# A gated layer's input projection, from plain products to a 2x2 block scheme with seven products

## The chip, the cores and the metric

The kernel runs on one core of a Trainium2 chip. The metric is the device time of one execution, in microseconds; the median of three runs is given. The trace is that of one execution taken by the hardware profiler. Of the core's engines, TensorE (PE) multiplies matrices into PSUM, VectorE (DVE), ScalarE (ACT) and GpSimd (POOL) work on elements, and SyncE (SP) issues the DMA transfers.

## The reference

Two batches, 512 "prompt" and 1024 "sample" tokens of 1024 features, go through two layers and a final norm. The first layer is multi-head latent attention. The second, which the change touches, is a chunked gMLP:

```python
def gmlp_layer(x, g, w_in, ln_g, ln_b, w_s, b_s, w_out):
    h = rmsnorm(x, g)
    u, v, gate = jnp.split(h @ w_in, 3, axis=-1)        # w_in: 1024 x 6144
    u = jax.nn.gelu(u, approximate=False)
    v = layernorm(jax.nn.gelu(v, approximate=False), ln_g, ln_b)
    vc = v.reshape(bsz, nc, 128, 8, 256)
    sv = jnp.einsum('gpq,bnqgd->bnpgd', w_s, vc) + jnp.transpose(b_s)[:, :, None]
    s = u * sv.reshape(bsz, seq, 2048)
    return x + (s * jax.nn.silu(gate)) @ w_out          # w_out: 2048 x 1024
```

All data is float32. Each large product is made of three: an operand is split into a rounded part (fp32r, "hi") and the remainder ("lo"), and hi*hi, hi*lo and lo*hi are summed in PSUM.

## The kernel before

Activations lie with features on the 128 partitions and tokens along the free axis. The 1536 tokens of the second layer ("layer B") are worked in three groups of 512: groups 0 and 1 are the sample batch, group 2 the prompt. The output projection of the attention layer (`AOut`, L719) writes its result to DRAM tiles `x1d`, one [128, 512] tile for each group and each of the eight feature tiles, and sums squares for the norm. `out_s` does groups 0 and 1, `out_p` (eight weight units of 24 products) group 2.

For each group, layer B then runs these stages:

- `b_prep` (L776): 1/rms of each token is spread over the partitions by small products (`start0`, `start`); `one(k)`, eight of them, loads a feature tile of `x1d` into a temporary (five buffers, tag `tmp`), scales it (L791) and splits it into `h2h` and `h2l`. Group 0's preparation is placed between the units of `out_p`, that of a later group between those of the output projection before it.
- `b_v` (L800): the 2048 features of v, with tokens on the partitions: the split activations are the stationary operand, weights of 512 columns the moving one; four column blocks x four units x four token tiles x two feature tiles x three products. Gelu, layer-norm statistics and the normalised v (`v2`) stay in SBUF.
- `b_ug` (L847): the 16 feature tiles of u and the 16 of the gate, in pairs: 24 products of 512 columns each (`mm3`, L132 to L134), then Gelu or Silu (L862). After each pair, `sp` (L866) mixes v over positions by small float32 products (L870), multiplies by u and gate and splits the result (`sf`).
- `b_out` (L887): output projection, 8 feature tiles x 48 products (L939 to L941), residual, squares; its final norm (`fin0` to `fin2`) is placed between steps of the next group's `b_v`.

Weights come as units of 512 KB (128 x 1024 float32) through the class `Weights` (L29): the DMA into `w_raw` (L43), rounded part by ACT (L50), remainder by DVE (L51), three buffers each. Units are split two ahead of use and loaded up to two ahead of that. Every DMA is issued on SP's queue.

The code is a list of steps (`step`, L113) that gives each instruction a priority; a planner then sets the order on each engine's queue, by what it expects to be ready, and each queue runs in that order, with a waiting instruction holding what stands behind it. Tiles share a fixed number of buffers by tag, and a new tile waits for a buffer of its tag. A pool that is opened after another is closed may lie on its addresses; its tiles then wait for those they overlap.

Of the kernel before, what the change touches and what calls it, by code (L numbers as in the profile page):

```python
# [22 lines left out]
C = 512  # L23
# [4 lines left out]

class Weights:  # L29
    """Stream of weight units: DRAM -> SBUF -> rounded part and remainder."""  # L30
# [8 lines left out]
    def _load(self, i):  # L39
        src = self.srcs[self.order[i]]  # L40
        n = src.shape[-1]
        t = self.pool.tile([128, 1024], F32, tag="w_raw", bufs=3, name="w_raw")
        self.nc.sync.dma_start(out=t[:, :n], in_=src)  # L43
        self.raw[i] = t, n
# [31 lines left out]
def trunk_kernel(tc, A):  # L76
# [24 lines left out]
    for d in range(16):  # L101
        srcs["wbu", d] = A["wbu"][d]
        srcs["wbg", d] = A["wbg"][d]
    for c in range(4):
        for u in range(4):
            srcs["wbv", c, u] = A["wbv"][c, u]
# [4 lines left out]
    prog = []          # (weight keys, function)  # L111
# [4 lines left out]
    st = {}            # state shared between steps  # L116

# [1 line left out]
    def mm_tile(name="mm"):  # L119
        return st["ps"].tile([128, C], F32, tag="mm", bufs=4, name=name)  # L120
# [7 lines left out]
    def mm3(out, terms):  # L128
        """sum of lhsT.T @ rhs over terms of (lhs hi, lhs lo, rhs hi, rhs lo)."""
# [54 lines left out]
    # the same in fewer dependent steps  # L184
# [36 lines left out]
    def setup():  # L221
        st["W"] = Weights(nc, open_pool("w", side="right"), srcs, order, 1, 3)
        st["ps"] = open_pool("psum", space=bass.MemoryType.PSUM)
# [11 lines left out]
        st["mhalf"] = const.tile([128, 4], F32, name="mhalf")  # L235
        dve.memset(st["mhalf"], -0.5)
        st["vec"] = const.tile([128, N_VEC], F32, name="vec")
# [16 lines left out]
    class AIn:  # L254
        """Input projection: latents (normalised, split), rotary key, gates."""
# [190 lines left out]
    def a_in_p(first):  # L446
        """-> (preparation steps, projection steps)"""
# [726 lines left out]
```

## Time and profile before

| | us |
|---|---|
| median of 3 runs | 2018.3 (2017.72 to 2018.39) |
| span of the profiled execution | 2016.2 |
| what lies around the span, taken from the two above | 2.1 |
| PE busy, share of the span | 1994.0, 99% |
| DVE busy | 1086.4, 54% |
| ACT busy | 813.4, 40% |
| DMA: bytes moved | 181.21 MB, mean 90 GB/s |

The profiled execution's own time is its span, 2016.2 us, and what lies around it, some 2.1 us. A busy PE is counted from the start of a product to its modelled end; products overlap, so the cost of one in a stream is the distance from start to start, and that is read from the order in time, not from the mean duration.

### The profile page before, as it was taken

Reading aid. Unit: us, or ns where it says so; the run is one execution under the profiler, and the core shown is the slowest. Engines: PE = TensorE matmul, PEld = TensorE weight load, DVE = VectorE, ACT = ScalarE, POOL = GpSimd, SP = SyncE. Lnnn points to the kernel's source line nnn. Section 1 sums busy time; section 2 is a strip of 40 time slices with the busy share of each in tenths; the row PEclk is TensorE's granted clock in tenths of the full one; section 3 lists DMA queues with packets and bytes.
Section 4 is the critical chain, followed back from the end, with each engine's and each line's share of the span. In section 5 each row is a group of like instructions: output and inputs, shape, how many; then the busy total and the mean of one; then the engine's idle time right before and its main releaser. Section 6 shows DMA issues by size and latency. Waiting matters only on the chain.

```text
span 2016.2 us, 24819 instructions
## 1 busy us (share of the span) xinstructions
PE 1994.0 (99%) x9984; PEld 1684.2 (84%) x9984; DVE 1086.4 (54%) x1580; ACT 813.4 (40%) x1207; POOL 134.4 (7%) x100
## 2 busy tenths in 40 slices
PE   8999999999999999999999999999999999999998
PEld 6888888888888888888888888888888888888887
DVE  7533777777856886255443445434444553434333
ACT  5323544545644654233244433323443332344421
POOL 4100000000110000220000001000000110000011
PEclk9999999999999999999999999999999999999999
DMA  4211000001113112463222234422223443222232
GB/s 157 84 44 55 22 18 16 22 21 38 48 53 107 53 61 86 143 216 121 94 94 94 87 107 157 141 95 94 93 84 105 146 142 109 94 94 84 94 120 100
DMA packets 65635, 181.21 MB, mean 90 GB/s; under 512 B 8048, under 2 KB 11632, under 8 KB 65520
## 3 DMA queue, kind: packets, MB, share of 16 engines
q1 hardware_dynamic: 65520, 179.63, 26.7%
q8 instruction: 78, 1.28, 0.3%
q14 instruction: 37, 0.30, 0.0%
HBM read 163.08 MB, written 12.58 MB: 87 GB/s over the span
## 4 chain that ended last, share of the span: by engine, by line
PE 95%; DVE 3%; issue 1%; ACT 1%; DMA 0%; POOL 0%; SPq 0%; POOLq 0%; DVEq 0%; ACTq 0%
PE mm L132 16%; PE mm L134 16%; PE mm L133 16%; PE s L581 9%; PE mm L941 4%; PE mm L940 4%; PE mm L939 4%; PE pst L613 3%; PE mm L828 2%; PE mm L826 2%; PE mm L827 2%; PE sv L870 2%; PE big L828 2%; PE big L826 2%; PE big L827 2%; PE o L133 2%
## 5 line engine op out<-in xcount | busy, mean ns | idle before, releaser
L51 DVE TENSOR_TENSOR w_lo<-w_raw,w_hi 128x1024 fp32r<-128x1024 f32 (+2 forms) x259 | 311.6, 1203 | 514.8 <-ACT w_hi L50 414.3
L50 ACT CAST w_hi<-w_raw 128x1024 fp32r<-128x1024 f32 (+2 forms) x259 | 266.4, 1029 | 643.2 <-PE mm L133 221.7
L132 PE MATMUL mm<-h2h,w_hi 128*128 128x512 f32 x768 | 300.9, 392 | 0.0
L134 PE MATMUL mm<-h2h,w_lo 128*128 128x512 f32 x768 | 298.9, 389 | 0.0
L133 PE MATMUL mm<-h2l,w_hi 128*128 128x512 f32 x768 | 298.8, 389 | 0.0
L212 POOL TENSOR_TENSOR acc<-acc,sq 128x512 f32<-128x512 f32 x70 | 107.9, 1542 | 1509.8 <-ACT sq L210 918.5
L134 PEld LDWEIGHTS mm<-h2h,w_lo 128*128 128x128 f32 x768 | 144.1, 188 | 30.4
L133 PEld LDWEIGHTS mm<-h2l,w_hi 128*128 128x128 f32 x768 | 144.2, 188 | 29.3
L132 PEld LDWEIGHTS mm<-h2h,w_hi 128*128 128x128 f32 x768 | 144.2, 188 | 29.2
L939 PE MATMUL mm<-sh,w_hi 128*128 128x512 f32 (+1 forms) x416 | 155.5, 374 | 0.0
L941 PE MATMUL mm<-sh,w_lo 128*128 128x512 f32 (+1 forms) x416 | 155.1, 373 | 0.0
L940 PE MATMUL mm<-sl,w_hi 128*128 128x512 f32 (+1 forms) x416 | 155.1, 373 | 0.0
L596 ACT ACTIVATE p<-s,sm 128x1024 f32<-128x1024 f32 (+1 forms) x96 | 93.2, 973 | 103.7 <-DVE sm L592 103.6
L132 PE MATMUL mm<-h_hi,w_hi 128*128 128x512 f32 x288 | 113.7, 395 | 1.1 <-ACT rbc L296 0.9
L137 ACT CAST pth<-pst 128x512 fp32r<-128x512 f32 x160 | 86.4, 590 | 67.2 <-PE pst L613 65.2
L134 PE MATMUL mm<-h_hi,w_lo 128*128 128x512 f32 x288 | 112.3, 390 | 0.0
L133 PE MATMUL mm<-h_lo,w_hi 128*128 128x512 f32 x288 | 112.1, 389 | 0.0
L138 DVE TENSOR_TENSOR ptl<-pst,pth 128x512 fp32r<-128x512 f32 x160 | 104.7, 682 | 8.4 <-ACT pth L137 8.3
L590 DVE TENSOR_REDUCE sm<-s 128x1 f32<-128x1024 f32 (+1 forms) x80 | 97.5, 1219 | 19.5 <-PE s L581 19.4
L133 PE MATMUL o<-ptl,vh 128*128 128x256 f32 x320 | 91.1, 285 | 0.0
L134 PE MATMUL o<-pth,vl 128*128 128x256 f32 x320 | 91.0, 284 | 0.0
L132 PE MATMUL o<-pth,vh 128*128 128x256 f32 x320 | 90.2, 282 | 0.0
(220 smaller groups left out, 3901.6 us busy)
## 6 DMA issues: line engine op xcount, KB each, us to landing
w_raw<-wbo SPq DMA_DIRECT2D x50, 512.0 KB, 3.6
w_raw<-wbv SPq DMA_DIRECT2D x48, 512.0 KB, 3.7
w_raw<-wbu SPq DMA_DIRECT2D x48, 512.0 KB, 3.6
w_raw<-wbg SPq DMA_DIRECT2D x48, 512.0 KB, 3.6
w_raw<-wa SPq DMA_DIRECT2D x25, 512.0 KB, 3.5
x<-x SPq DMA_DIRECT2D x48, 256.0 KB, 2.9
x<-xs SPq DMA_DIRECT2D x32, 256.0 KB, 3.1
w_raw<-wao SPq DMA_DIRECT2D x16, 512.0 KB, 3.8
```

The lines of the kernel that those rows point to most:

```text
L50: self.nc.scalar.copy(hi[:, :n], raw[:, :n])
L51: self.nc.vector.tensor_tensor(out=lo[:, :n], in0=raw[:, :n], in1=hi[:, :n].bitcast(F32), op=ALU.subtract)
L132: pe.matmul(out, lh, rh, start=(i == 0), stop=False)
L133: pe.matmul(out, lh, rl, start=False, stop=False)
L134: pe.matmul(out, ll, rh, start=False, stop=(i == n - 1))
L138: dve.tensor_tensor(out=lo, in0=src, in1=hi.bitcast(F32), op=ALU.subtract)
L212: pool_e.tensor_tensor(out=acc, in0=acc, in1=s, op=ALU.add)
L581: pe.matmul(s[:, j2 * C:(j2 + 1) * C], l[:, o], r[:, cc], start=(j == 0), stop=(j == 4))
L590: dve.tensor_reduce(out=sm[:, 0, :], in_=s.rearrange("p (a b) -> p a b", a=ns), axis=AX.X, op=ALU.max)
L939: pe.matmul(ps, wh[:, ksl(kk)], sh, start=(k == 0), stop=False)
L940: pe.matmul(ps, wh[:, ksl(kk)], sl, start=False, stop=False)
L941: pe.matmul(ps, wl[:, ksl(kk)], sh, start=False, stop=(k == 15))
```

## The change

The input projection of layer B is made of 2x2 blocks: the contracted features are halved (512 and 512), the output features are halved, and the tokens are halved. The four output blocks then come from seven block products of sums and differences of blocks, not from eight plain ones. The tokens are worked in two groups of 768 (so that half a group, `H`, is 384).

- The seven left factors are A11, A12, A22 of the weights and four sums S1 to S4. The sums don't depend on tokens; `w_sums(u)` makes them on the chip, 24 times: it loads 1 MB of weights into one tile, makes four [128, 512] results on DVE and stores 1 MB to DRAM. Four of these stand between the units of `out_p`, 14 in the first group's v stage, 6 in its u and gate stage.
- The seven right factors are made by `b_prep`, now four steps `one(k)` for each group: two loads of 768 tokens, one after the other through one buffer (`hx`), two scalings into `hQ` (one buffer), four subtractions of 384 columns, a store of three factors to DRAM (`gbd`), a split of the other four (1536 columns). `b_prep2` reloads and splits the three during v.
- `b_v`: for each group two halves of features, seven products, four feature tiles, three token tiles, three matmuls: 504 of 512 columns. `b_ug`: 16 units x 7 x 4 x 3 = 1344 of 384 columns.
- `gather` puts the products together: three of the seven are copied by ACT out of PSUM while the bank goes on being summed into (`held`), three results are the sum of a bank and such a copy (DVE).
- v goes to DRAM and comes back normalised for each pair of feature tiles (`load_v`); s goes to DRAM (`sd`) and is loaded and split in groups of 512 tokens for the output projection (`s_load`), whose first two feature tiles are interleaved by halves.
- PSUM has two tags of four banks in layer B.
- A weight unit is now two pieces of [128, 512]; 84 units for each group (168 in all, where there were 144), some loaded by two DMAs.

Of the diff, the new parts that carry work (`...` marks what is left out):

```diff
+    def w_sums(u):
+        def fn():
+            raw = st["ws"].tile([128, 4, C], F32, tag="ws_raw", bufs=1, name="ws_raw")
+            sm = st["ws"].tile([128, 4, C], F32, tag="ws_sum", bufs=1, name="ws_sum")
...
+            nc.sync.dma_start(out=raw, in_=src)
+            for o, a, b, op in ((sm[:, 1], raw[:, 2], raw[:, 3], ALU.add),
+                                (sm[:, 0], sm[:, 1], raw[:, 0], ALU.subtract),
+                                (sm[:, 2], raw[:, 0], raw[:, 2], ALU.subtract),
+                                (sm[:, 3], raw[:, 1], sm[:, 0], ALU.subtract)):
+                dve.tensor_tensor(out=o, in0=a, in1=b, op=op)
+            nc.sync.dma_start(out=dst, in_=sm)
+    def b_prep(G):
...
+        def one(k):
+            def fn():
+                Q = st["hq"].tile([128, 7, H], F32, tag="hQ", bufs=1, name="hQ")
+                for j in range(2):
+                    x = st["hq"].tile([128, 2 * H], F32, tag="hx", bufs=1, name="hx")
...
+                        nc.sync.dma_start(out=x[:, t0 - 2 * H * G:t0 - 2 * H * G + n],
+                                          in_=st["x1d", g, k + 4 * j][:, o:o + n])
...
+                    dve.scalar_tensor_tensor(
+                        out=Q[:, j:j + 5:4, :], in0=x.rearrange("p (a b) -> p a b", a=2),
...
+                for o, a, b in ((3, 4, 0), (2, 5, 3), (4, 5, 4), (6, 1, 2)):
+                    dve.tensor_tensor(out=Q[:, o, :], in0=Q[:, a, :], in1=Q[:, b, :], op=ALU.subtract)
+                nc.sync.dma_start(out=st["gbd", G, k], in_=Q[:, 4:7, :].rearrange("p a b -> p (a b)"))
...
+                split(hl[0], hl[1], Q[:, 0:4, :].rearrange("p a b -> p (a b)"))
...
+    def gather(i, ps, keep, new, n, sink):
+        X, Y, Z = (ps.get(r) for r in "XYZ")
+        def held(src):
+            t = new("t")[:, :n]
+            act.copy(t, src[:, :n])
+            return t
+        if i == 0:
+            keep["t1"] = held(X)
+        elif i == 1:
+            sink(0, 0, keep.pop("t1"), Y[:, :n])
+        elif i == 2:
+            keep["t2"] = held(X)
+        elif i == 3:
+            keep["t5"] = held(Z)
+        elif i == 4:
+            sink(1, 1, keep.pop("t5"), X[:, :n])
+        elif i == 5:
+            sink(0, 1, keep.pop("t2"), Z[:, :n])
+        else:
+            sink(1, 0, None, X[:, :n])
...
+        def unit(n, func, outs):
...
+                    for k in range(4):
+                        chain3(banks[BANK[i]][:, :H], (wh[:, ksl(k)], wl[:, ksl(k)]), right(i, k),
+                               k == 0 and i in (0, 1, 3), k == 3)
+                    gather(i, banks, keep, new, H, sink)
...
-    prep = [b_setup] + b_prep(0) + [b_bias(0), b_bias(1)]
+    prep = [b_setup] + b_prep(0) + [w_sums(i) for i in range(4)] + [b_bias(0), b_bias(1)]
...
-        for _ in range(2 if f else 0):
+        for _ in range(3 if f else 0):
             if prep:
                 step(prep.pop(0))
...
+    todo_w = list(range(4, 24))
+    for G in range(2):
+        step(open_in)
+        v, prep2 = b_v(G), b_prep2(G)
+        for i, s in enumerate(v):
+            step(*s)
+            if i % 4 == 3 and prep2:
+                step(prep2.pop(0))
+            if G == 0 and i % 4 == 1 and todo_w:
+                step(w_sums(todo_w.pop(0)))
+        step(open_ug)
...
+        for g in ((0,), (1, 2))[G]:
+            for d in range(16):
+                step(s_load(g, d))
+            fin = b_out(g, b_prep(1) if g == 0 else (list(fin) if g == 2 else []), g == 2)
```

The banks of the seven products are `BANK = "XYXZXZX"`: X is summed into by products 0, 2, 4 and 6, with a copy (0, 2) or an addition (4) that reads it in between.

## Rows read from the trace of the kernel before

**Rows 1.** Page, parts 1 and 4: span; shares of the chain that ended last.
```profile
span 2016.2 us, 24819 instructions
...
PE 95%; DVE 3%; issue 1%; ACT 1%; DMA 0%; POOL 0%; SPq 0%; POOLq 0%; DVEq 0%; ACTq 0%
```

**Rows 2.** Stages by windows: length, busy us (instructions) by engine, PE clock, DMA share, GB/s.
```profile
862.00:907.00 45.00, 45.00 (x198) 36.83 (x197) 28.34 (x38) 17.03 (x24) 12.48 (x10) 1.00 0.64 220
911.00:998.00 87.00, 87.00 (x386) 71.98 (x385) 38.29 (x57) 27.21 (x35) 2.94 (x4) 1.00 0.34 112
998.00:1186.60 188.60, 188.60 (x898) 158.44 (x897) 81.64 (x97) 80.27 (x95) 1.88 (x1) 1.00 0.27 90
1186.60:1273.60 87.00, 87.00 (x385) 72.02 (x384) 44.03 (x49) 26.80 (x34) 10.00 (x6) 1.00 0.43 145
2001.40:2016.20 14.80, 6.04 (x49) 5.68 (x47) 5.86 (x16) 0.42 (x1) 0.71 (x1) 0.78 0.41 142
```

**Rows 3.** Groups by shape: line, engine, tiles, count, busy us, mean ns, idle before.
```profile
L132 PE MATMUL mm<-h2h,w_hi 128*128 128x512 f32 x768 | 300.9, 392 | 0.0
L133 PEld LDWEIGHTS mm<-h2l,w_hi 128*128 128x128 f32 x768 | 144.2, 188 | 29.3
L870 PE MATMUL sv<-wsT,v 128*128 128x128 f32 x384 | 46.7, 275 | 0.0
```

**Rows 4.** Chain in order of time (start, us, what): two mixes, one pair apart, group 0.
```profile
1019.66 1.78 PE sv L870 x16
...
1043.24 1.78 PE sv L870 x16
```

**Rows 5.** PE in order of time: first and last of 21 products of 256 columns.
```profile
299.93 0.28 PE L132 MATMUL mm<-w_hi,lat4h 128*128 128x256 f32 x1
...
302.33 0.28 PE L134 MATMUL mm<-w_hi,lat4l 128*128 128x256 f32 x1
```

**Rows 6.** Groups by shape, DVE and ACT: what the new element work resembles.
```profile
L51 DVE TENSOR_TENSOR w_lo<-w_raw,w_hi 128x1024 fp32r<-128x1024 f32 x235 | 289.8, 1233 | 513.5 <-ACT w_hi L50 413.2 <-PE sv L870 99.8
L50 ACT CAST w_hi<-w_raw 128x1024 fp32r<-128x1024 f32 x235 | 247.1, 1052 | 620.4 <-PE mm L133 200.8 <-issue 188.5 <-PE mm L940 100.8
L137 ACT CAST pth<-pst 128x512 fp32r<-128x512 f32 x160 | 86.4, 590 | 67.2 <-PE pst L613 65.2 <-DVE qr L547 1.8
L879 DVE TENSOR_TENSOR sv<-sv,ug 128x512 f32<-128x512 f32 x48 | 30.9, 685 | 0.0
```

**Rows 7.** POOL, SP and DVE in order of time: norm factor, a load of `one(k)`, its scaling.
```profile
880.76 0.19 POOL L750 COPY r<-rstd 128x4 f32<-128x4 f32 x1
...
882.08 0.37 SPq L790 DMA_DIRECT2D x<-x  x1
...
885.20 0.75 DVE L791 SCALAR_TENSOR_TENSOR x<-x,vec,rbc 128x512 f32<-128x512 f32 x1 [2.19 <-DMA x<-x]
```

**Rows 8.** PE in order of time: where `out_p` ends and v begins.
```profile
909.09 0.39 PE L134 MATMUL mm<-goh,w_lo 128*128 128x512 f32 x1
...
909.77 0.80 PE L826 MATMUL big<-w_hi,h2h 128*128 128x512 f32 x1
```

**Rows 9.** DMA issues (count, KB each, median us to landing) and the densest window.
```profile
w_raw<-wbv SPq DMA_DIRECT2D x48, 512.0 KB, 3.7
x<-x SPq DMA_DIRECT2D x48, 256.0 KB, 2.9
...
890.00:900.00 10.00, 10.00 (x45) 8.27 (x45) 8.52 (x10) 4.82 (x7) 1.91 (x2) 1.00 0.80 269
```

**Rows 10.** DVE in order of time at the end of group 0's `b_ug`.
```profile
1189.28 1.29 DVE L880 TENSOR_TENSOR sv<-sv,ug 128x512 f32<-128x512 f32 x2
1190.48 0.69 DVE L180 TENSOR_TENSOR dg<-ident,r 128x512 f32<-128x512 f32 x1
1191.08 1.29 DVE L138 TENSOR_TENSOR sl<-sv,sh 128x512 fp32r<-128x512 f32 x2
```

**Rows 11.** Waits of SP's queue: the longest in total (us, times, longest).
```profile
SPq L43 <- DVE w_lo L51: 1409.2, 244, 38.1
```

More of the change, by code (lines that the diff above doesn't have):

```diff
@@ L40, in _load @@
         src = self.srcs[self.order[i]]
-        n = src.shape[-1]
+        parts = src() if callable(src) else [src]
         t = self.pool.tile([128, 1024], F32, tag="w_raw", bufs=3, name="w_raw")
-        self.nc.sync.dma_start(out=t[:, :n], in_=src)
+        n = 0
+        for a in parts:
+            self.nc.sync.dma_start(out=t[:, n:n + a.shape[-1]], in_=a)
+            n += a.shape[-1]
         self.raw[i] = t, n
@@ L794, in fn, with b_prep2 @@
+                st["ga", k] = hl
+            return fn
+        return [rb0(0), rb0(1), rb1(0), rb1(1)] + [one(k) for k in range(4)]
+    def b_prep2(G):
+        def one(k):
+            def fn():
+                x = st["h2b"].tile([128, 3 * H], F32, tag="gbx", bufs=1, name="gbx")
+                nc.sync.dma_start(out=x, in_=st["gbd", G, k])
+                hl = [st["h2b"].tile([128, 3 * H], F32R, tag=f"gb{e}{k}", bufs=1, name="gb" + e)
                       for e in "hl"]
                 split(hl[0], hl[1], x)
-                st["h2", k] = hl
+                st["gb", k] = hl
@@ new lines, in b_prep2, with right, bank, chain3 @@
+        return [one(k) for k in range(4)]
+    def right(i, k, o=slice(0, H)):
+        t, j = (st["ga", k], i) if i < 4 else (st["gb", k], i - 4)
+        return [a[:, j * H + o.start:j * H + o.stop] for a in t]
+    def bank(role):
+        return st["ps"].tile([128, C], F32, tag="x" if role == "X" else "y", bufs=4, name=role)
+    def chain3(ps, lhs, rhs, first, last):
+        (lh, ll), (rh, rl) = lhs, rhs
+        pe.matmul(ps, lh, rh, start=first, stop=False, skip_group_check=True)
+        pe.matmul(ps, lh, rl, start=False, stop=False, skip_group_check=True)
+        pe.matmul(ps, ll, rh, start=False, stop=last, skip_group_check=True)
@@ new lines, in mix, with end, fn @@
+            return fn
+        def end(p, u, g):
+            def fn():
+                for e in range(2):
+                    dve.tensor_tensor(out=u[e], in0=u[e], in1=g[e], op=ALU.mult)
+                    nc.sync.dma_start(out=st["sd", G, 2 * p + e], in_=u[e])
+            return fn
+        step(load_v(0))
+        for p in range(8):
+            u, g = [], []
+            unit(2 * p, AF.Gelu, u)
+            if p < 7:
+                step(load_v(p + 1))
+            for e in range(2):
+                step(mix(p, u, e))
+            unit(2 * p + 1, AF.Silu, g)
+            step(end(p, u, g))
@@ new lines, in s_load, with fn @@
+    def s_load(g, d):
+        def fn():
+            x = tmp("s")
+            t0 = g * C
+            while t0 < (g + 1) * C:
+                G, o = divmod(t0, 2 * H)
+                n = min(2 * H - o, (g + 1) * C - t0)
+                nc.sync.dma_start(out=x[:, t0 - g * C:t0 - g * C + n], in_=st["sd", G, d][:, o:o + n])
+                t0 += n
+            hl = [st["po"].tile([128, C], F32R, tag=f"s{e}{d}", bufs=1, name="s" + e) for e in "hl"]
+            split(hl[0], hl[1], x)
+            st["sf", d] = hl
+        return fn
@@ L970, in b_out @@
                     step((lambda: half_norm(0, st["hsq"])) if u == 0 else lambda: half_scale(0))
-            for e in extra[:1 if i < 2 else 2]:
-                step(e)
-            extra = extra[1 if i < 2 else 2:]
+                for e in extra[:1]:
+                    step(e)
+                extra = extra[1:]
         if last:
@@ L1055, in open_b3 @@
         close_pool("outp")
         close_pool("gatep")
-        st["b3"] = st["ap"] = open_pool("b3")
-        st["acc_n"] = 2
-    step(open_b3)
-    for g in range(3):
-        if g:
-            v = b_v(g)
-            for i in range(3):
-                steps(v[i:i + 1])
-                step(fin[i])
-            steps(v[3:])
-        b_ug(g)
-        fin = b_out(g, b_prep(g + 1) if g < 2 else [], g == 2)
+        close_pool("psum")
+        st["ps"], st["mm"] = open_pool("psumb", space=bass.MemoryType.PSUM), "y"
```

354 lines of the change are left out of this document (226 added, 128 removed).

## The prediction, as put on record before the changed kernel ran

> **What bounds the kernel now.** First the page: the span, and the chain that ended last, of which PE holds 95% [rows 1]; DVE has 3%, DMA none. Then the windows by stage [rows 2]: in v (911 to 998), u and gate (998 to 1186.6) and output (1186.6 to 1273.6) PE is busy for the whole stretch at the full granted clock, DVE for 43 to 51% of it, and the DMA engines for 27 to 43%. So in layer B a product less is its time less, as long as nothing else becomes late. The exception to keep in mind is the stretch just before v, 862 to 907: DVE is busy for 28.3 of 45 us and the DMA share is 0.64 [rows 2]. That is the place with the least cover, and the change puts work there.
>
> **What a product costs.** The order in time gives it. Two mixes stand one pair apart, at 1019.66 and 1043.24, and the mix takes 1.78 [rows 4]; the 96 products of 512 columns between them take 21.80 us, 0.2271 each. Products of 256 columns start 2.40 us apart over 20 steps, 0.1200 each [rows 5]. The 384 columns of the new u and gate products are not in the trace; midway between the two it is 0.1736, and I take that, since both neighbours lie on the same slope (0.42 ns a column and 13 ns fixed).
>
> **What the products give.** u and gate: 3 x 768 = 2304 of 512 columns before [rows 3], 523.2 us; after, 2 x 1344 = 2688 of 384, 466.6 us; 56.6 less. v: 1152 of 512 columns before, 1008 after, 144 x 0.2271 = 32.7 less. The mixes stay 384 instructions, and the output projection stays. Together **89.3 us**, all of it on the path. The rest of the sum is how much of that is lost to stalls of PE.
>
> **The new preparation, ahead of v.** `one(k)` now forms a chain, since its load and its result have one buffer each. The factor for group 1 is ready at 880.95, and spread over partitions some 3.5 us later [rows 7]: start 884.5. Per k, by the nearest rows: the scaling of 768 columns 1.1 (0.75 for 512), the second load 3.5 (3.1 from issue to scaling for 256 KB), a second scaling 1.1 [rows 7], four subtractions of 384 columns 4 x 0.55 (0.685 for 512 and 1.233 for 1024 give 1.07 ns a column) [rows 6], the store of 576 KB 3.8 [rows 9], beside which the split runs (ACT 1.5 and DVE 1.8 by [rows 6]), and 0.4 between engines: 12.1 us until the next k may write. The last k's split parts are there at 884.5 + 3 x 12.1 + 11.4 = 932. PE has finished `out_p` and begins v at 910 [rows 8]; its first product needs k = 0 to 3 in turn, and the fourth is due 27 products later, at 916. That is a stall of 16 us, and the lower end. The DMA engines make it longer: in its densest window the trace has 269 GB/s at a share of 0.80 [rows 9], 336 GB/s if all are busy. The stretch 862 to 907 moved 220 x 45 us = 9.9 MB [rows 2]; the change adds four weight sums at 2.1 MB, 2.4 MB of stores and 1 MB of loads, 21.7 MB or 65 us in a stretch of 48. With loads of 7 and stores of 8 us behind that queue a k takes 19.8 and the stall is 44. I take 4.5 and 5.5 (the queue is not full all the time): 14.8 for each k, ready at 941, a stall of **25 us** (16 to 44). PE waits in pieces there. The one idle end of the trace shows what the clock then does: a mean of 0.78 in 2001 to 2016, with PE busy for 6 of 14.8 us [rows 2], so partly at the lower level, 1.2 GHz. If the 27 products between the waits run at half speed that is 6 us; I take **3** (0 to 6).
>
> **The weight sums under v and u.** 24 sums, each a load of 1 MB (2.0 us fixed from a 512 KB load's 3.7 [rows 9], and 3.1 of moving: 5.1), 4 x 0.685 on DVE, and a store. From `out_p` to the end of the first group's u and gate stage PE has about 46 + 114 + 255 = 415 us of work (8 x 24 products and small ones; 504; 1344 and half the mixes). DVE has there: `out_p` and preparation 48; v 28 x 1.23 of weight remainders, 42 x 0.69 of additions and statistics, 5 of reloads: 69; u and gate 56 x 1.23, 48 x 0.55, 32 x 0.56 and 32 x 0.96 of mixing, 14 of normalising: 158; the sums 66. That is 341 of 415, with 74 idle. If the sums are ready when DVE comes to them, nothing is lost; if each holds DVE's queue for its load, 24 x 5.1 = 122, less the 74 idle, 48 are lost. Weights need not starve: their loads mostly wait for a free buffer now, 1409 us in all [rows 11], so they come early and have a reserve. In v the DMA engines would be asked for 14.7 MB of weights, 6.3 of v, 2.4 of factors and, if as fast as written, 29 of sums, 157 us at 336 GB/s against 114 of PE; but sums for u are not due until u, and may lag by 100 us. I take **10 us** (0 to 48), nearest to the present rows, where the planner's order leaves DVE little waiting for DMA.
>
> **Hand-overs in PSUM.** X is summed into again one product after it was read, so ACT's copy (or DVE's addition) has 12 x 0.1736 = 2.08 us. The copy of 384 columns takes about 0.48 (0.590 for 512), and one cast of a weight unit ahead of it 1.05 [rows 6]: 1.5 with 0.3 of hand-over is 1.8. It fits, with no more than one such piece ahead; in v the window is 8.2. Small losses are within the next item.
>
> **The changes of stage.** At each end of u and gate, s goes through DRAM: a store, a load and a split, 8 us for the last tiles, which are due only 2 x 24 products = 10.9 us into the output stage thanks to the interleaved halves; the early tiles lie on buffers in use to the end, 3 to 4 us. From v to u about 1, twice; the final norm of group 0 has no step of v written between its parts (0 to 5, since the planner may start v's products meanwhile); four buffers for six held copies in v, about 1 us four times. Sum **10 us** (3 to 25).
>
> **The sum.** The profiled execution: 2016.2 - 89.3 + 25 + 3 + 10 + 10 = 1974.9, and the 2.1 us by which the median stands above this span: **1977 us**. Its own range is 1950 to 2013: the low end has the 16 and the 3 and little else, the high end two of the upper bounds at once.
>
> **Rivals.**
> *The queues hold what waits at their heads; slower.* If the order on DVE and SP is close to the order of the code, each `one(k)` (12.4 with its loads behind a waiting store) and each of the first four sums (5.1 + 2.75 + half a store, 11) runs one after the other, and the weight remainders of `out_p`'s last units stand behind them: 884.5 + 4 x 12.4 + 4 x 11 = 978, then two units of 24 products, v at 989 instead of 910: 79 lost, with 3 for the clock, 20 under v and u and 10 at the changes of stage: 2018.3 - 89.3 + 112 = **2041**. It decides for slower once all stalls together pass 89. For it: SP's stores do wait at the head, and these are new chains with one buffer. Against: the planner doesn't keep the code's order; the norm factor of the next group (L180, written after the first output step) runs on DVE ahead of the last split of s (L138) [rows 10].
> *The preparation is hidden.* Loads and sums begin as early as their buffers allow, PE loses 5 before v and 8 elsewhere: **1942**. Against: the factor at 881 and the one-buffer chain behind it don't depend on the order.
> *A product of 384 columns doesn't get its share.* A weight load is recorded with 188 ns [rows 3]; the line through 0.1113 for 128 columns (1.78 over 16 [rows 4]) and 0.2271 for 512 gives 0.1885 for 384. Then u and gate save only 16.5, all products 49.2, and the time is 2018.3 - 49.2 + 48 = **2017**, no change. Against it stands the 0.1200 for 256 columns, with a load before each product [rows 5]. The Trainium skill, "TensorE: Matmul & The Clock Gate", Back-to-back issue gap, speaks for such a fixed part: in streams of loads and products it gives 81 ns at 128 columns and 131 at 512, so an estimate of 114 at 384, by which 2688 smaller products would cost more than 2304 large ones; the trace doesn't agree, its products of 512 start 227 ns apart.
>
> **How the numbers follow.** Forecast 0.60, hidden 0.12, no share 0.06, queues 0.22. A measurement of this kernel tells 0.2% (4 us) from no change: faster 0.72, same 0.06, slower 0.22. The range leaves out half of the hidden case and rather more than half of the queue case, which reaches past 2041: **1943 to 2035**.
>
> **What would show it.** Right: u and gate products start 0.174 apart, v's 0.227; the idle time of PE is mostly ahead of v's fourth weight piece, behind DVE's split of `ga`, with the DMA share above 0.8 there; stretches of u and gate near 255 us, the second group's free of idle time. Wrong: if v begins near 985 with `out_p`'s last units late behind w_lo, it is the queues; if products start 0.188 apart, the weight load; if PE waits in u for `t` copies in each unit, the hand-over, which I put at nothing.

## The result, and the profile after

The changed kernel takes **2053.0 us** (2051.6 to 2056.4 over 4 runs) against 2018.35 before: ratio 1.0175, 95% interval 1.0161 to 1.0190. It is slower, by 34.7 us, and above the whole forecast range. The profiled execution spans 2049.8 us, 33.6 more than before.

From the page of the changed kernel: span, then the DMA share and GB/s in 40 slices of 51 us, then the chain that ended last. Against [rows 1] PE's share of the chain falls from 95 to 82%, and DVE and DMA come in; five slices in a row stand at 0.9 or more.

```profile
span 2049.8 us, 26616 instructions
...
DMA  4211000001123113478999995456565654535452
GB/s 155 83 43 55 21 18 16 22 21 47 37 72 93 47 68 108 136 254 282 321 328 328 314 318 174 144 192 205 179 225 172 198 178 162 170 129 179 136 203 98
...
PE 82%; DVE 7%; DMA 6%; ACT 2%; issue 2%; POOL 1%; SPq 0%; POOLq 0%; DVEq 0%; ACTq 0%
```

Its stages by windows, columns as in [rows 2]: ahead of v, then v, u and gate, output of the first group, and u and gate of the second.

```profile
907.00:963.00 56.00, 21.18 (x71) 14.24 (x70) 42.03 (x65) 11.09 (x12) 9.76 (x5) 0.68 0.86 288
963.00:1094.00 131.00, 124.73 (x505) 97.78 (x506) 87.77 (x115) 55.45 (x72) 1.20 (x2) 0.95 0.91 320
1094.00:1365.80 271.80, 259.25 (x1537) 256.43 (x1535) 180.90 (x261) 129.18 (x173) 1.32 (x1) 0.98 0.70 239
1365.80:1461.00 95.20, 92.37 (x388) 73.78 (x389) 63.61 (x72) 35.32 (x46) 8.68 (x6) 0.98 0.62 204
...
1587.00:1845.00 258.00, 255.15 (x1537) 254.49 (x1535) 158.96 (x223) 128.24 (x171) 2.26 (x1) 1.00 0.52 168
```

Cut at the first product of each stage in PE's order of time, the 33.6 us are:

| stretch | before | after | difference |
|---|---|---|---|
| start to `out_p`, code not touched | 863.9 | 869.8 | +5.9 |
| `out_p` to v's first product | 45.9 | 93.6 | +47.7 |
| v, u and gate, all groups | 830.8 | 786.7 | -44.1 |
| output projections and end | 275.6 | 299.7 | +24.1 |

Half of the 89 us saved on products arrived. Two entries stand out: the stretch ahead of v, and the first, where nothing was changed.

**Ahead of v.** PE in order of time; in brackets how long it was idle before the row, and what ended that.

```profile
928.38 2.07 PE L787 MATMUL rs<-wsT,ones 128*128 128x512 f32 x2 [17.57 <-DVE ones L786]
939.93 2.08 PE L787 MATMUL rs<-wsT,ones 128*128 128x512 f32 x2 [9.48 <-DVE ones L786]
962.09 0.80 PE L175 MATMUL ps_n<-sh,onesr 128*128 128x512 f32 x1 [7.77 <-ACT sh L146]
```

PE names a memset of 0.17 us. What it waited for stands in front of that memset in DVE's queue:

```profile
918.75 1.02 DVE L882 SCALAR_TENSOR_TENSOR hQ<-hx,vec,rbc 128x768 f32<-128x768 f32 x1 [3.27 <-DMA hx<-x]
...
923.58 1.29 DVE L814 TENSOR_TENSOR ws_sum<-ws_raw 128x512 f32<-128x512 f32 x2
...
928.16 0.17 DVE L786 MEMSET ones<- 128x128 f32 x1
933.02 1.02 DVE L882 SCALAR_TENSOR_TENSOR hQ<-hx,vec,rbc 128x768 f32<-128x768 f32 x1 [4.70 <-DMA hx<-x]
...
951.74 1.75 DVE L147 TENSOR_TENSOR gal<-hQ,gah 128x1536 fp32r<-128x1536 f32 x1
```

Scalings that wait for their loads, additions of weight sums, splits of `ga`: a chain of DVE and DMA. The last two units of `out_p` stand behind `rs` on PE and end at 953.9, v begins at 963.4. The granted clock of the window is 0.68, so part of the time at the lower of the two levels, 1.2 GHz, after PE had been idle in pieces. The rows show what that costs: v's first products start 0.43 us apart, not 0.2333.

```profile
963.41 0.63 PE L918 MATMUL X<-w_hi,gah 128*128 128x512 f32 x1
963.84 0.63 PE L919 MATMUL X<-w_lo,gah 128*128 128x512 f32 x1
```

From 869 to 968, 29 products start late in this way, 5.7 us in all.

**Where nothing was changed.** PE in the first layer, the first product of four units of 24 in turn:

```profile
803.63 0.40 PE L141 MATMUL mm<-goh,w_hi 128*128 128x512 f32 x1
...
809.11 0.40 PE L141 MATMUL mm<-goh,w_hi 128*128 128x512 f32 x1
...
814.71 0.40 PE L141 MATMUL mm<-goh,w_hi 128*128 128x512 f32 x1
...
820.18 0.40 PE L141 MATMUL mm<-goh,w_hi 128*128 128x512 f32 x1
```

These are 5.48, 5.60 and 5.47 us from start to start, 0.2283, 0.2333 and 0.2279 a product in turn, with no wait. Before, all such units took 5.44, 0.2267 a product. The units differ in the pool of `go`: one chunk of tokens lies in `outs0` on the right side of SBUF, the other in `outs1` on the left. The change altered sizes in `const` (one tile `r1` in place of three small ones), and every tile behind it on the left side starts 32 bytes lower.

**The 384 columns** came as forecast: 30 products from the first to the second row in 5.20 us, 0.1733 each.

```profile
1639.83 0.34 PE L920 MATMUL X<-gah,w_lo 128*128 128x384 f32 x1
...
1645.03 0.34 PE L920 MATMUL Z<-gah,w_lo 128*128 128x384 f32 x1
```

### The profile page after: what moved, and what is told of

Same layout as the page of the kernel before. It is cut to its first block, busy times and chain, and to the rows that moved or that the text cites. A ratio compares the mean times of both kernels' runs of the same rounds, so it can differ in the third digit from the quotient of the medians.

```text
span 2049.8 us, 26616 instructions
## 1 busy us (share of the span) xinstructions
PE 1954.3 (95%) x10226; PEld 1701.7 (83%) x10226; DVE 1288.2 (63%) x1918; ACT 885.7 (43%) x1341; POOL 133.3 (7%) x99
## 4 chain that ended last, share of the span: by engine, by line
PE 82%; DVE 7%; DMA 6%; ACT 2%; issue 2%; POOL 1%; SPq 0%; POOLq 0%; DVEq 0%; ACTq 0%
PE s L591 8%; PE mm L141 7%; PE mm L142 7%; PE mm L143 7%; PE X L919 5%; PE X L918 5%; PE X L920 5%; PE mm L1143 4%; PE mm L1142 4%; PE mm L1144 4%; PE pst L623 3%; PE Z L919 3%; PE Z L918 3%; PE Z L920 3%; PE sv L1046 2%
## 5 line engine op out<-in xcount | busy, mean ns | idle before, releaser
L62 ACT CAST w_hi<-w_raw 128x1024 fp32r<-128x1024 f32 (+2 forms) x283 | 290.4, 1028 | 547.8 <-PE mm L142 126.8
L63 DVE TENSOR_TENSOR w_lo<-w_raw,w_hi 128x1024 fp32r<-128x1024 f32 (+2 forms) x283 | 342.4, 1212 | 214.6 <-ACT w_hi L62 213.7
L1143 PE MATMUL mm<-sl,w_hi 128*128 128x512 f32 (+1 forms) x416 | 160.4, 386 | 5.4 <-DVE sl L147 5.2
L1142 PE MATMUL mm<-sh,w_hi 128*128 128x512 f32 (+1 forms) x416 | 159.8, 384 | 5.8 <-ACT sh L146 5.8
L1143 PEld LDWEIGHTS mm<-sl,w_hi 128*128 128x128 f32 x416 | 79.5, 191 | 24.6 <-DVE sl L147 8.6
L1142 PEld LDWEIGHTS mm<-sh,w_hi 128*128 128x128 f32 x416 | 79.4, 191 | 23.1 <-ACT sh L146 6.9
L918 PE MATMUL X<-gah,w_hi 128*128 128x384 f32 x256 | 88.5, 346 | 6.7 <-ACT w_hi L62 6.7
L1144 PEld LDWEIGHTS mm<-sh,w_lo 128*128 128x128 f32 x416 | 79.6, 191 | 15.9
L918 PE MATMUL X<-gbh,w_hi 128*128 128x384 f32 x256 | 86.6, 338 | 3.8 <-DVE uo L1015 3.8
L920 PE MATMUL X<-gah,w_lo 128*128 128x384 f32 x256 | 87.2, 341 | 0.3 <-DVE w_lo L63 0.3
```

The source lines that it names most:

```text
L62: self.nc.scalar.copy(hi[:, :n], raw[:, :n])
L63: self.nc.vector.tensor_tensor(out=lo[:, :n], in0=raw[:, :n], in1=hi[:, :n].bitcast(F32), op=ALU.subtract)
L918: pe.matmul(ps, lh, rh, start=first, stop=False, skip_group_check=True)
L920: pe.matmul(ps, ll, rh, start=False, stop=last, skip_group_check=True)
L1142: pe.matmul(ps, wh[:, ksl(kk)], sh, start=(k == 0), stop=False)
L1143: pe.matmul(ps, wh[:, ksl(kk)], sl, start=False, stop=False)
```

## Experiments: where the operands start

Two theories: the slower cadence comes from where a product's two operands start, or it comes along with the transfers.

`b_shift`, the kernel before with one line more:

```diff
+        const.tile([128, 8], F32, name="pad")
         st["vec"] = const.tile([128, N_VEC], F32, name="vec")
```

> The kernel before with one unused tile of 32 bytes ahead of `vec` in `const`: every tile of the pools on the left side moves up by 32 bytes, nothing else changes. In the changed kernel the products of 512 columns start 0.2333 us apart, in the kernel before 0.2267, in the first layer too, which the change doesn't touch; there the tiles behind `const` lie 32 bytes lower than before, by its changed sizes. Theory 'placement': what counts is where the two operands of a product start, modulo 64 bytes; with the shift the products of the first layer and of the output projection (1152) start 0.2333 apart, v, u and gate (both operands on the right side, not moved) stay at 0.2267. That is 6 for the first layer, 1 for out_p, 1152 x 0.0066 = 7.6 for the output: 2033. Theory 'traffic or clock' (the slower cadence comes with the changed kernel's transfers or its load): no change, 2018.

Measured: **2031.6** (ratio 1.0067, 1.0052 to 1.0082), 13.4 us more for 32 unused bytes. Its first layer has the pattern of the changed kernel, 5.60 and 5.48 us:

```profile
809.37 0.40 PE L132 MATMUL mm<-goh,w_hi 128*128 128x512 f32 x1
...
814.97 0.40 PE L132 MATMUL mm<-goh,w_hi 128*128 128x512 f32 x1
...
820.45 0.40 PE L132 MATMUL mm<-goh,w_hi 128*128 128x512 f32 x1
```

v, u and gate, whose operands didn't move, stayed at the old cadence: 276.5 us from v to output, as before. So it is placement, not traffic.

`a_align` puts the changed kernel's tiles back by 32 bytes on both sides, `a_place2` also takes the tile `mv` out of `b2`, so that `ga` starts at the same remainder as the weights (first edit `a_align`, the others `a_place2`; both with the line of `b_shift`):

```diff
         bp = st["b2"] = open_pool("b2", side="right")
+        bp.tile([128, 8], F32, name="pad2")
...
         st["h2b"] = open_pool("h2b", side="right")
+        st["mv"] = st["h2b"].tile([128, 6, 4], F32, name="mv")
...
-            mv = st["mv"] = st["b2"].tile([128, 6, 4], F32, tag="mv", bufs=1, name="mv")
+            mv = st["mv"]
```

> The changed kernel with one unused tile of 32 bytes in `const` and one in `b2`, so that the tiles on both sides start again at the remainder of 32 that the weight tiles have. Theory 'placement': all products of 512 columns 0.2267 apart, 0.0066 less each: 6 in the first layer, 1 in out_p, 2016 x 0.0066 = 13 in v and output, about 20 in all: 2033. The stalls ahead of v stay. Theory 'traffic or clock': 0.2333 stays, 2053.

> The changed kernel with an unused tile of 32 bytes in `const` (as in a_align) and the tile `mv` moved from `b2` to the start of `h2b`, so that `ga` and `gb` start at the remainder 480 of 512 bytes, the one of the weight tiles; in a_align it was 352, in the changed kernel 384. There v's products started 0.2323 apart with 352, 0.2333 with 384, and the 384-column ones 0.1760 and 0.1733. Theory 'difference': what counts is the distance between the starts of the two operands modulo 256 bytes, and distance 0 is the fastest, as in the kernel before (h2 at 480): v 0.2267 apart, u and gate 0.1733 or less; against a_align 1008 x 0.0056 = 5.6 and 2688 x 0.0027 = 7.3 less: 2036. Theory 'half line' (only the remainder of 64 bytes counts): as a_align, 2049.

Measured: 2048.8 and **2043.9** (1.0109 to 1.0139). First layer and output return to 0.2267 in both. v tells the theories apart; 30 products of the changed kernel, then of `a_place2`:

```profile
969.80 0.39 PE L918 MATMUL X<-w_hi,gah 128*128 128x512 f32 x1
...
976.80 0.39 PE L918 MATMUL Y<-w_hi,gah 128*128 128x512 f32 x1
```

```profile
969.81 0.39 PE L919 MATMUL Y<-w_hi,gah 128*128 128x512 f32 x1
...
976.61 0.39 PE L919 MATMUL X<-w_hi,gah 128*128 128x512 f32 x1
```

0.2333 and 0.2267; in `a_align`, which has the right remainder of 64 but not of 512, 0.2320, and its 384-column products went to 0.1760 (0.1733 in the other two). So 'half line' is out, and the distance of the two starts counts. By the addresses in the programs as built, 0 bytes modulo 256 (0 and 256 of 512) gave 0.2267 in every stream looked at (0.228 where such units alternate with slower ones), distances of 32 and 96 gave 0.2333, 128 gave 0.2320. What happens inside was not tried. The Trainium skill, "SBUF — State Buffer", Who interferes with whom, gives TensorE two independent read ports, for the moving operand and for the weight load, and says that it never waits on anyone. The section speaks of engines that disturb each other; if it held between the two operands of one engine as well, their placement would cost nothing, and these traces, 0.2333 against 0.2267, don't agree with that.

Only 9 of the 21 us came back. The first layer and the output got shorter; v stayed nearly as long as it was (128.7 us in the first group, 125.5 in the second), and u and gate of the first group took 274.2: PE waits there in any case.

## Experiments: the weight sums

`a_nosums` leaves the sums out, `a_traffic` only their additions (the store sends the loaded block), `a_adds` only their transfers (in this order in the diff):

```diff
         def fn():
+            return
...
-                dve.tensor_tensor(out=o, in0=a, in1=b, op=op)
-            nc.sync.dma_start(out=dst, in_=sm)
+            nc.sync.dma_start(out=dst, in_=raw)
...
-            nc.sync.dma_start(out=raw, in_=src)
...
-            nc.sync.dma_start(out=dst, in_=sm)
```

> The changed kernel without the weight sums: no loads, additions and stores for them, and the products that take a sum of weight blocks take a block itself, so this part of the result is left out; the number and form of the products stays. Theory 'the sums' transfers': from 905 to 1220 us the DMA engines are busy for more than 0.9; without the 48 transfers a k of the preparation takes 12 instead of 14 us, v begins 8 to 15 earlier, and the waits for weights in the first group's v and u (about 13 and 14) go: 2053 - 35 = 2018 (2010 to 2028). Theory 'chain and queue' (the one-buffer chain of the preparation and the order on PE set the stall, and the waits in v and u come from the change of stage): 2045 to 2053.

> The changed kernel with the loads and stores of the 24 weight sums but without their additions: the store sends the loaded blocks themselves, so this part of the result is left out. The products read them as before. Without sums altogether the time was 2007.6, 45 less. Theory 'transfers': the DMA engines' load sets the loss, the additions (24 x 2.75 us of DVE) little: 2043 to 2053. Theory 'DVE queue': the additions wait at the head of DVE's queue for their loads, and the scalings, evacuations and weight remainders stand behind them: without them 2010 to 2020.

> The other half: the changed kernel with the 96 additions, on one tile that is loaded once, and without the other loads and all stores of the weight sums; the products take a weight block where they took a sum, so this part of the result is left out. Theory 'transfers': close to the kernel without sums, 2008 to 2014. Theory 'DVE queue' in the form that the work itself (66 us) is what is missing on DVE: 2030 to 2050; in the form that DVE stands waiting for the loads, which are gone here: 2008 to 2014 as well, so that a_traffic tells this form from the transfers.

Measured: **2007.6** without sums (45 less, more than either theory had), **2041.8** without additions (11 less), **2015.3** without transfers (38 less). The two halves add up to 49, so they hardly share. Counted from the kernel without sums, the transfers alone cost 34 us and the additions alone 8. Stretches in us, by the first products:

| | `out_p` to v | v | u and gate | (second group) v | u and gate |
|---|---|---|---|---|---|
| changed kernel | 93.6 | 130.6 | 271.9 | 125.8 | 258.4 |
| `a_nosums` | 68.4 | 118.9 | 259.1 | 125.7 | 259.0 |
| `a_traffic` | 87.4 | 125.8 | 269.3 | 125.3 | 258.8 |
| `a_adds` | 78.1 | 119.6 | 258.7 | 127.7 | 263.2 |

The sums cost 25 us ahead of v, 12 in v and 13 in u and gate, 50 together; without them the output stages and the end took some 4 more, which makes the 45. Windows of v, without sums and with their transfers alone:

```profile
938.00:1057.00 119.00, 119.00 (x504) 95.63 (x505) 66.79 (x78) 56.17 (x73) 1.21 (x2) 0.99 0.57 187
```

```profile
957.00:1082.60 125.60, 120.44 (x505) 94.87 (x504) 63.80 (x76) 55.46 (x72) 1.21 (x2) 0.99 0.92 332
```

DVE has the same work in both, 66.8 and 63.8 us, and PE has no gap in the first. With the DMA engines at 0.92 and 332 GB/s a sum's load of 1 MB landed after 6.7 to 8.0 us in the median, and PE waited for `w_hi`. The loads of v's weights slowed down with them: a unit of 512 KB landed after 3.4 us in the median without sums, after 6.2 to 6.7 with their transfers alone and after 8.1 to 8.2 in the changed kernel (the first line is without sums, the second the changed kernel):

```profile
w_raw<-wv SPq DMA_DIRECT2D x22, 512.0 KB, 3.4
```

```profile
w_raw<-wv SPq DMA_DIRECT2D x8, 512.0 KB, 8.2
```

One rival stays open. Every DMA is issued on SP's queue, and there the sums' stores wait for their data: 75.6 us in 18 waits from 963 to 1220 in the changed kernel, 62.8 in 14 in `a_traffic`, with the weight loads behind them. Full engines and a held queue both went with the transfers in `a_nosums` and `a_adds`; no run took away one of them alone.

## Experiments: what else holds v back

Without sums 22.5 us stay ahead of v. Three edits to the changed kernel look for a wait of its own.

`a_bias` makes `ones` once, `a_prep2` gives the preparation two buffers (`hx` likewise), `a_late` moves the norm's last step:

```diff
-            ones = tmp("ones")[:, :128]
-            dve.memset(ones, 1.0)
...
-                Q = st["hq"].tile([128, 7, H], F32, tag="hQ", bufs=1, name="hQ")
+                Q = st["hq"].tile([128, 7, H], F32, tag="hQ", bufs=2 - G, name="hQ")
...
-    step(lambda: out_p.stats(0))
...
+            if G == 0 and i == 12:
+                step(lambda: out_p.stats(0))
```

> The changed kernel with the tile of ones for the two bias products made once in the set-up of the layer, as in the kernel before, instead of in a temporary tile ahead of each product. In the changed kernel PE waits 17.6 and 9.5 us ahead of these products for DVE's memset, which stands in DVE's queue behind the scalings that wait for their loads; the last two units of out_p stand behind the products on PE. Theory 'the head of DVE's queue': the waits go, out_p ends at about 919 instead of 954, and v is then held by the fourth k of the preparation, whose split was ready at 953.5: its 28th product starts there instead of at 969.7, 16 less: 2037. Theory 'the preparation alone' (PE would have waited for it all the same): the idle time only moves ahead of v, 0 to 6 less, 2047 to 2053.

> The changed kernel with two buffers instead of one for the preparation's load `hx` and its result `hQ` in the first group. Theory 'one-buffer chain': a k takes 14 us because each load waits for the scaling ahead of it and each k for the store ahead of it; with two buffers it falls to 8 to 9 (DVE's own 6.5, transfers of 1.35 MB), the last split is ready 15 to 18 earlier, and v begins as much earlier: 2035 to 2038. Theory 'transfers': the engines are full already (share 0.85 from 905 to 963), a k takes 12 to 14 as before, or the sums' loads give way: 2045 to 2053.

> The changed kernel with the last step of the norm of the last chunk of `out_p` (the two products `ps_n` and what follows) moved from ahead of v to behind v's 12th weight piece; its result is needed only by the second group. In the changed kernel PE waited 7.8 us for `ps_n` just before v, since the PSUM pools change there and every older PSUM tile must be done. Theory 'a wait of its own': v begins right behind out_p at about 955, all `ga` parts are ready at 955.3: 7 to 8 less, 2045. Theory 'it stands for DVE's queue' (v's first weights or `ga` come late by as much): 0 to 3 less.

Measured: 2057.5, 2060.1 and 2050.8: two lose, and `a_late` gains 2, within the spread of its runs, where a wait of its own had been worth 7 to 8. In `a_bias` the waits for `ones` are gone and stand elsewhere:

```profile
928.17 0.77 PE L141 MATMUL mm<-goh,w_hi 128*128 128x512 f32 x1 [8.80 <-DVE x L746]
...
962.55 0.79 PE L175 MATMUL ps_n<-sh,onesr 128*128 128x512 f32 x1 [26.14 <-ACT sh L146]
```

`a_prep2` shows most. The last split of `ga` is done at 926.9, 26 us earlier than in the changed kernel, and v begins at 965.1, later than there. DVE, in order of time:

```profile
925.12 1.76 DVE L147 TENSOR_TENSOR gal<-hQ,gah 128x1536 fp32r<-128x1536 f32 x1 [0.60 <-ACT gah L146]
933.72 1.29 DVE L814 TENSOR_TENSOR ws_sum<-ws_raw 128x512 f32<-128x512 f32 x2 [6.84 <-DMA ws_raw<-wv]
...
936.79 0.30 DVE L786 MEMSET ones<- 128x128 f32 x2
946.51 1.29 DVE L814 TENSOR_TENSOR ws_sum<-ws_raw 128x512 f32<-128x512 f32 x2 [9.41 <-DMA ws_raw<-wv]
```

Now the sums stand at the head of DVE's queue and wait for their loads, and with them the memset and the evacuations that PE needs. So the chain alone was not the bound. The rows put DVE's queue in its place, whichever instruction stood at its head; no run shortened that queue alone. In `a_late` PE waited for an evacuation (`x`) instead of the norm, and v began 6 us earlier, counted from `out_p`'s start, but v took 136.5 us instead of 130.6.

## Experiments: the sums in another place

If the price is the place, sums made in the first layer (DMA share 0.07 to 0.25, POOL idle) cost nothing. `a_early` makes them there, in 96 pieces on POOL, with the placement of `a_place2`:

```diff
+            raw, sm = (tmp(n).rearrange("p (a b) -> p a b", a=4) for n in ("ws_raw", "ws_sum"))
-                dve.tensor_tensor(out=o, in0=a, in1=b, op=op)
+                pool_e.tensor_tensor(out=o, in0=a, in1=b, op=op)
...
+    weave += [(2 + i * 4 // 5, f) for i, f in enumerate(ws[:68])]
     main_s(weave, [mm_p[0], mm_p[2]])
```

> The changed kernel with the placement of a_place2, and with the weight sums made in the first layer: 96 pieces of 128 columns, loaded into temporary tiles, added on POOL and stored, between the score blocks of the attention (200 to 780 us), where the DMA share is 0.07 to 0.25 and POOL is nearly idle. Nothing is left out. Theory 'transfers at the wrong place': what the sums cost was their place; in the first layer they cost nothing. Then the time is that without sums, 2007.6, less the placement (6 in the first layer, 1 in out_p, 7 in v, 7 in the output): 1987 (1982 to 1995). Theory 'the transfers cost wherever they are': temporary buffers, POOL beside DVE and the queue of SP hold the attention up by 0.2 to 0.4 us a piece, 19 to 38: 2006 to 2025.

> a_early with two buffers for the preparation's load `hx` and its result `hQ` in the first group. With the sums beside it this brought nothing (a_prep2, 7 slower). Without sums a k of the preparation took 12.1 us and DVE was busy for 26.9 of 33 us there. Theory 'one-buffer chain': now that the transfers are away the period falls to DVE's own work, 8 to 9 us, the fourth k is ready 10 to 14 earlier, v begins as much earlier: 1973 to 1978. Theory 'DVE's work': 0 to 5 less than a_early.

> a_early2 with the ones for the bias products made once in the set-up (a_bias). With the sums beside it that moved the wait of PE behind the products and gained nothing. Theory 'it only moves': within 3 of a_early2. Theory 'head of DVE's queue': without the sums the order on PE counts, out_p's last units come 5 to 9 earlier: 4 to 8 less than a_early2.

Measured: **2016.9** (0.9977 to 0.9997 of before), 2021.7 and 2021.0. The first is in the range of 'the transfers cost wherever they are'. Behind the first layer `a_early` has what was hoped: v 116.1, u and gate 259.7. But `out_p` begins at 889.6 instead of 864.4 in `a_place2`, so the pieces cost 25 us in the first layer, 15 of them in two waits, at the change of attentions and in the second one (the 14 in the next expectation is too small a count):

```profile
539.28 1.97 PE L628 MATMUL pst<-ident,p 128*128 128x128 f32 x8 [7.61 <-DVE p L619]
...
767.58 0.90 PE L628 MATMUL pst<-ident,p 128*128 128x128 f32 x3 [7.71 <-DVE ql L147]
```

In `a_early2` a k takes 8 us in the mean, and the last split ends at 942.8; PE still waits for `rs` and `ps_n`, and v begins at 963.6: 5 us slower, not 10 to 14 faster. With the transfers away, too, the one-buffer chain alone is not the bound, and in `a_early3` the wait for `ones` only moves again.

`a_early4` puts the pieces elsewhere, `a_early5` adds `a_late` and `a_bias`, `a_early6` moves the preparation's subtractions to POOL:

> a_early with the pieces of the sums at other places of the first layer: 18 in the input projection and 78 between the first 50 score blocks, none near the change from one attention to the other and none in the second one, where PE stood for 7.8 us twice in a_early. Theory 'place': the two stalls and most of the 14 us go: 2001 to 2006. Theory 'the pieces cost wherever they are': 2013 to 2017.

> a_early4 with the norm's last step behind v's 12th piece (a_late) and the ones made once (a_bias). Theory 'waits of their own': 9.5 for `ps_n` and 8.4 for `rs` were PE's waits in a_early; both gone, v is held by the last k alone (15 us between its split and v's first product in a_early2): 10 to 16 less than a_early4. Theory 'DVE's queue': evacuations and weight remainders of out_p's last units are late by as much: 0 to 5 less.

> a_early5 with the preparation's four subtractions on POOL in the first group and two buffers for `hx` and `hQ` there. From 909 to 943 DVE was busy throughout in a_early2, 34 us for four k. Theory 'DVE's work is what is left': 2.2 x 4 = 9 us go from DVE, two buffers let POOL work beside it: 6 to 10 less than a_early5. Theory 'transfers and order': 0 to 3 less, or more time where POOL's slower subtractions lengthen the chain.

Measured: 2019.6, 2016.2 and 2024.3. `a_early4` met neither of its theories: `out_p` begins at 893.5, since PE is 15 us behind `a_place2` early in the first attention, by the pieces in the input projection, and 29 behind at its end. `a_early5` gives 3.4, as 'DVE's queue' has it: ahead of v it gains 9.2 (58.5 against 67.7), but v takes 123.6 instead of 116.3. In `a_early6` the last split is done 16 us earlier than in `a_early5`, and v begins 7 later; DVE was not relieved (45.3 us busy from `out_p` to v against 40.8). A scaling in `a_early2`, where POOL didn't run, and one in `a_early6` beside POOL's subtractions:

```profile
919.75 1.01 DVE L885 SCALAR_TENSOR_TENSOR hQ<-hx,vec,rbc 128x768 f32<-128x768 f32 x1
```

```profile
928.38 4.66 POOL L893 TENSOR_TENSOR hQ<-hQ 128x384 f32<-128x384 f32 x3 [1.33 <-DVE hQ L887]
...
930.40 1.77 DVE L887 SCALAR_TENSOR_TENSOR hQ<-hx,vec,rbc 128x768 f32<-128x768 f32 x1
```

1.01 became 1.77, and a subtraction takes 1.0 to 2.5 on POOL against 0.55 on DVE. The Trainium skill, "SBUF — State Buffer", Who interferes with whom, says that a DVE instruction with two SBUF inputs contends with a POOL instruction that reads SBUF; the trace agrees, with 1.77 for 1.01.

`a_early7` keeps the pieces away from the places that lost, and leaves nine sums whole and on DVE; the code has them in the first group's u and gate stage, where their pool is opened:

```diff
+NE = 15
+    ws = [w_sums(u, c) for u in range(NE) for c in range(4)]
+    weave += [(1 + i * 47 // len(ws), f) for i, f in enumerate(ws)]
     main_s(weave, [mm_p[0], mm_p[2]])
...
-    todo_w = list(range(4, 24))
+    todo_w = list(range(NE, 24))
```

> The changed kernel with the placement of a_place2, the norm's last step as in a_late, the ones as in a_bias, and the weight sums in two parts: the first 15 in 60 pieces between the first 48 score blocks of the first attention (none in the input projection, where a_early4 lost 15 us, none at the change of attentions and in the second one, where a_early lost twice 7.8), the other nine, needed late in u and gate, whole and on DVE in the first group's u and gate stage. Nothing is left out. Theory 'place': the first layer loses at most 5 against a_place2, the nine late sums at most 5: 2016.9 - 14 - 3 + 5 = 2005 (2000 to 2010), faster than the kernel before. Theory 'the pieces cost wherever they are': 9 to 18 lost in the first layer and 5 to 10 in u and gate: 2011 to 2022.

Measured: **1996.7** (1993.9 to 1997.8), ratio 0.9888 (0.9871 to 0.9904): faster than the kernel before by 21.5 us and than the changed one by 56, with all of its work done, and below the range of both theories. The first 15 sums between the score blocks cost next to nothing (`out_p` begins at 866.1 against 864.4), `a_place2` first and `a_early7` second:

```profile
200.00:500.00 300.00, 299.47 (x1851) 264.64 (x1850) 226.22 (x400) 149.41 (x266) 0.00 (x0) 1.00 0.08 22
```

```profile
200.00:500.00 300.00, 298.26 (x1843) 263.21 (x1842) 228.96 (x396) 147.77 (x263) 121.26 (x240) 1.00 0.44 127
...
907.00:930.00 23.00, 10.04 (x32) 7.40 (x30) 21.58 (x35) 6.00 (x6) 3.77 (x2) 0.76 0.65 211
930.00:1053.00 123.00, 119.76 (x505) 97.79 (x506) 82.82 (x107) 58.59 (x76) 4.53 (x3) 0.96 0.81 288
```

The other nine didn't run where the code has them. SP's queue shows the first of their loads 3.4 us after v's first product, at 930.1:

```profile
933.54 0.33 SPq L816 DMA_DIRECT2D ws_raw<-wug  x1
...
953.05 0.79 SPq L816 DMA_DIRECT2D ws_raw<-wug  x1
```

Six of the nine loads were issued during v, the last one at 1097.6, 20 us apart in the mean where the changed kernel's came 14 apart. Beside them the DMA share in v is 0.81, a weight load of v landed after 4.2 to 4.5 us, PE waited for no weight, and v took 123.2 us against 123.6 in `a_early5`, which has no sums there; u and gate took 260.8 against 261.0. So nine sums at this pace, beside v and u, cost little.

v begins 64.0 us after `out_p`. In the last 23 us of that DVE is busy for 21.6: what stays of the stall, 18 us more than before, is, by this row, DVE's work and its order. How much of it is work and how much order was not taken apart.

## Why the prediction was wrong, step by step

- **What a product costs, 384 columns: right.** 0.1733 against 0.1736. The rival 'doesn't get its share' (0.1885) is out. The Trainium skill, "TensorE: Matmul & The Clock Gate", Back-to-back issue gap, gives 81 ns at 128 columns and 131 at 512 for streams of loads and products; these traces don't agree, with 173 ns at 384 and 227 to 233 at 512. u and gate of the second group took 258.4, near the 255.
- **What a product costs, 512 columns: wrong**, and it was not taken for a step at all. "The output projection stays", and layer A wasn't named. At 0.2333 for 0.2267 this is 6 in the first layer, 1 in `out_p`, 1008 x 0.0066 = 7 in v and 1152 x 0.0066 = 8 in the output: **21 us** that the sum didn't have. `b_shift` shows the cause. In the changed kernel, where v waits in any case, `a_place2` got only 9 of them back.
- **The preparation ahead of v: the size was near, the mechanism wrong.** 25 and 3 were forecast; without sums it is 22.5, with a k every 12.2 us, near the 12.1 worked out for an unloaded queue, and 14 to 16 with sums. But the stall doesn't end with the last split of `ga`: `a_prep2` and `a_early2` had that 38 and 21 us before v's first product. By the rows it ends when DVE's queue has passed the evacuations, the bias products' `ones` and the norm.
- **The weight sums: the term that failed most**, 10 forecast, **45** measured. The step was "sums for u are not due until u, and may lag by 100 us". They didn't lag, they came as early as their buffers let them: all 24 one after the other, 14 us each, 882 to 1219, and the DMA engines were full for v and half of u. The forecast had worked out the demand (157 us of transfers against 114 of PE in v) and then put it aside. It also took the reserve in SP's waits [rows 11] for one that a full queue would leave in place: SP's waits for `w_lo` from 963 to 1220 fell from 229.9 to 51.1 us, and a weight load of v took 8.2 us instead of 3.4. And it weighed DVE's free time, when the transfers alone cost 34 of the 45.
- **The clock: near.** 3 (0 to 6) was forecast; 29 products at the lower level cost 5.7 us at most, since waits follow many of them. The granted clock of 0.68 over 56 us looks worse than it is, since PE was busy for only 21 of them.
- **Hand-overs in PSUM: right**, 1.3 us of waits for DVE's additions in u and gate of the second group, 2.4 in the first.
- **Changes of stage: too small.** 10 forecast. The output and the end took 24.1 more, 16.5 without the cadence, and 11 of that are PE's waits for the split of s at the starts of the output stages. v of the second group took 125.8 against 504 x 0.2333 = 117.6, 8 more, some 5 of them in waits: for the norm 2.2, for weights 1.8, for the reloaded `gb` 1.2. About 25 together, the upper end. No experiment touched these.
- **The rivals.** 'The queues hold what waits at their heads' was the nearest of the four times with 2041, and right in that sums and preparation share one stretch of DVE's queue ahead of v. It put 79 there, and 48 were lost, 22.5 of them without any sums. Its sign, `out_p`'s last units late behind w_lo, didn't come: they stood behind the bias products. The reason against it, that the planner doesn't keep the code's order, was the wrong way round: the planner moved the sums forward, beside the preparation.
- **The whole.** Some 123 us were lost, the 89.3 that were to be saved and 33.6 on top. The sums have 45 of them, the preparation with the clock 22.5, the changes of stage 25, the cadence 9 to 21; 10 to 20 are not placed.

## What to carry to other kernels

Work that is due late isn't done late by itself: unless its buffers or its inputs come late, it runs as early as it can, beside the most urgent work, so a sum of free engine time over a whole stage says little; put it where DMA and DVE are idle, or thin it out (15 sums in the first attention and nine beside v and u, 20 us apart, were nearly free; 24 of them 14 us apart, from ahead of v on, cost 45 us). If the wait that a profile names is removed and the time doesn't move, look at what stands in front of the named instruction in its queue. And compare the pace of streams that a change doesn't touch before you add anything up: a few bytes in an early pool move every tile behind it.

## What the runs showed of the hardware

The start of a 512-column product after the one before depends on where its two operands lie: 0.2267 us when they start a multiple of 256 bytes apart, 0.2333 and 0.2320 at distances of 32 or 96 and of 128; the 384-column ones took 0.1733 at 0 and 96 and 0.1760 at 128. 32 unused bytes cost the kernel before 13.4 us of 2018. At the lower level of the clock the 512-column products started 0.43 us apart. DVE's scaling of 768 columns took 1.01 us alone and 1.77 beside POOL's subtraction.
